# Two pairs of experts summed in one accumulation group, and expert weights loaded as runs of consecutive rows

## The chip, the cores and the metric

The kernel runs on one core of a Trainium2 chip. The metric is the device time of one execution in microseconds (us), with all inputs in HBM at the start and the output in HBM at the end. Three runs of the kernel before took 1796.16, 1798.23 and 1798.26 us; the median is 1798.23.

## The reference

The kernel computes two transformer blocks over 512 tokens of width 1024 in float32. The change touches the mixture of experts at the end of the first block. Cut to what matters, it is:

```python
def hierarchical_moe(h, w_rg, b_rg, w_re, b_re, w_gate, w_up, w_down):
    xt = h.reshape(512, 1024)
    ...                                   # top-1 group of 4, then top-2 of its 8 experts
    def expert_block(args):               # rows of one expert: 1024 -> 512 -> 1024
        toks, e = args
        xb = x_pad[toks]
        hid = jax.nn.silu(xb @ w_gate[e]) * (xb @ w_up[e])
        return hid @ w_down[e]
    ...
    out = out.at[tok_buf].add(y * w_buf)  # each token: the sum over its two experts
```

The kernel reads every expert's three matrices (2 MiB each, 192 MiB in all) once. `h` is the RMS norm of the residual `x` with gain `ffn_norm_g`, and the result is added to `x`.

## The kernel before, in words

The kernel is one stream of work built in program order for five engines. TensorE's order is fixed by `chained` (L154): every matmul is tied behind the one emitted before it. Weights and other inputs are loaded by DMAs that SyncE issues in order.

The stage of the experts runs from about 303 us to 814 us of the profile. The 32 experts are taken as 16 pairs, numbered p = 0 to 15, and two pairs (p even, then p odd) share one one-hot matrix and one gathered input. Each expert has 64 slots for tokens. The steps of a pair are methods of the class `Experts`:

- `dispatch` (L1096) gathers the tokens of two pairs by multiplying the residual rows, held as a high part `xh` and a low part `xl`, with the one-hot matrix `oh`. It is done in two halves of 512 features, each evicted by VectorE with the norm's gain.
- `gate` (L1132) and `up` (L1155) multiply the gathered input with the expert's weights. Expert 0 of the pair uses columns 0 to 63 of TensorE's array and expert 1 columns 64 to 127, in plain float32, so two matmuls run side by side. Each has 8 chunks k of 128 input features.
- `hidden` (L1165): ScalarE makes the silu of the gate from PSUM (through `act`, L188), and VectorE multiplies it with the up part (L1169) into `sg`.
- `turn` (L1171) transposes `sg` on TensorE into `hT`; `down` (L1179) multiplies it with the down weights, and ScalarE and VectorE split the result into a high and a low part (`split`, L143).
- `prepare` (L1138) transposes the next pair's one-hot into `ohT` and collects its token weights.
- `adds` (L1190) scatters a pair's rows back: for each of 8 chunks m of output features two matmuls of the full 128x128 array with `ohT`, and one VectorE addition into the residual `x1T` (L1199).

The main loop (L1438) interleaves them. While pair p runs its `up`, the eight adds of pair p-1 are dropped in one at a time after chunks 1 to 7 of the up sweep, and the eighth behind it. Between `hidden` and `turn`, and between `turn` and `down`, TensorE is given other work (`fill`): the next pair's gate in two halves if p is even, the two halves of the next dispatch if p is odd, and for p = 15 two adds each time. The adds of the last pair run after a test for overflowing experts (L1468).

The expert weights are loaded 1 MiB at a time into a ring of 13 tiles (`ring`, L879), which reuses all of the kernel's weight buffers. A load can be issued once the matmuls that read the tile's last contents are done. `load_up` (L889) gives partition p of chunk k the input row 128 k + p of the expert, a run of 2 KB; `load_down` (L894) likewise, with runs of 4 KB. `got_o` (L927) makes `xh` and `xl` before the stage, on ScalarE (L953) and GpSimd (L958).

Of the kernel before, what the change touches and what calls it, by code (L numbers as in the profile page):

```python
# [18 lines left out]
P = 128  # L19
# [20 lines left out]
def _program(tc, nc, es, I, out):  # L40
# [20 lines left out]
    def a4(shape, dt=F32):  # L61
        return ap_.tile(shape, dt, tag="a", name=nm("a"))
# [16 lines left out]
    def b32(ap):  # L79
        return ap.bitcast(F32)  # L80
# [253 lines left out]
    for g in range(4):  # L334
        nc.sync.dma_start(w_r[:, :, 4 + 8 * g:12 + 8 * g],
                          I["w_router_expert"][0, g].rearrange("(k p) e -> p k e", p=P))
    b_r = rp_.tile([P, 36], F32, name="b_r")
    nc.sync.dma_start(b_r[:, 0:4], I["b_router_group"][0].partition_broadcast(P))
    nc.sync.dma_start(b_r[:, 4:36], I["b_router_expert"][0].rearrange("g e -> (g e)").partition_broadcast(P))

# [545 lines left out]

    wg_d, wu_d, wd_d = I["w_gate"][0], I["w_up"][0], I["w_down"][0]

    def load_up(src, e, half):  # L889
        w = wtile([P, 4, FF])  # L890
        nc.sync.dma_start(w, src[e, half * 512:(half + 1) * 512, :].rearrange("(k p) f -> p k f", p=P))
        return w

    def load_down(e, half):  # L894
        w = wtile([P, 2, D])
        nc.sync.dma_start(w, wd_d[e, half * 256:(half + 1) * 256, :].rearrange("(k p) f -> p k f", p=P))
        return w

    def loads():
# [13 lines left out]
    emb_d = dr.tile([P, NT, D], F32, name="emb_d")  # L913

    ss1 = tm.tile([P, NT, 4], F32, name="ss1", bufs=1)
    xh, xl, x1T = [], [], []
    lt_ps = pvb()
    posts = []

# [7 lines left out]
    def got_o(g, c2, ps):  # L927
        xx = xt[g][:, 2 * c2:2 * c2 + 2, :]
        V.tensor_tensor(xx, xx, ps, op=ALU.add)

        def post():
            if len(x1T) == g:
                x1T.append(a4([P, 2, S]))
                xh.append(a4([P, NT, 256], F32R))
                xl.append(a4([P, NT, 256], F32R))
            ts = slice(c2 * 256, c2 * 256 + 256)
            pt = tr((P, 2, 256))
            for k in range(2):
                for ci in range(2):
                    tpose(pt[:, k, ci * P:(ci + 1) * P], xt[g][:, 2 * c2 + ci, k * P:(k + 1) * P])  # L940
            xr[:] = [tm.tile([P, 2, 256], F32R, tag=t, name=nm("xr"), bufs=b) for t, b in (("ohT", 2), (("sg", "hT")[c2], 1))]
            hi = nc.scalar.activation(xr[0], pt, AF.Copy)
            V.tensor_tensor(xr[1], pt, b32(xr[0]), op=ALU.subtract)
            cs = slice(2 * c2, 2 * c2 + 2)
            rest, last_ = [], (g, c2) == (3, 1)
            for ci in range(2):
                c = 2 * c2 + ci
                junk = tm.tile([P, 256], F32, tag="junk", name=nm("junk"), bufs=1)
                rest.append(nc.scalar.activation(junk, xt[g][:, c, :], AF.Square, accum_out=ss1[:, c, g:g + 1]))
            if last_:  # L950
                rms1()
            more = [nc.scalar.activation(x1T[g][:, :, ts], pt, AF.Copy),
                    nc.scalar.activation(xh[g][:, cs, :], xx, AF.Copy)]  # L953
            for i_ in rest:
                tc.add_manual_dep(i_.ins, hi.ins.name, no_sync, reason="order")
            for i_ in more:
                tc.add_manual_dep(i_.ins, rest[-1].ins.name, no_sync, reason="order")
            i_ = nc.gpsimd.tensor_tensor(xl[g][:, cs, :], xx, b32(xh[g][:, cs, :]), op=ALU.subtract)  # L958
            if last_:
# [136 lines left out]
    def dispatch(oh, nsl, XT):  # L1096

        per = 512 // nsl if nsl >= 128 else 4  # L1100
        for half in range(2):
            X = a4([P, 4, nsl])
            for k0 in range(0, 4, per):
                ps = mm((P, per, nsl))
                for kk in range(per):
                    k = half * 4 + k0 + kk
                    for c in range(NT):
                        mmul(ps[:, kk, :], xh[k // 2][:, c, (k % 2) * P:(k % 2 + 1) * P], oh[:, c, :], c == 0, False)
                        mmul(ps[:, kk, :], xl[k // 2][:, c, (k % 2) * P:(k % 2 + 1) * P], oh[:, c, :], False, c == NT - 1)
                k = half * 4 + k0  # L1110
                V.tensor_tensor(X[:, k0:k0 + per, :], ps,
                                gffn[:, k:k + per, :].broadcast_to([P, per, nsl]), op=ALU.mult)
            XT.append(X)
            yield

    class Experts:


        def __init__(self, XT, s0, ne, wg, wu, wd, oh_pair, g_of, after=None):
            self.XT, self.s0, self.ne, self.n = XT, s0, ne, ne * SLOTS  # L1120
            self.wg, self.wu, self.wd, self.oh, self.g_of, self.after = wg, wu, wd, oh_pair, g_of, after
            self.rows = []

        def _up(self, ps, w, ks):
            for k in ks:
                for e in range(self.ne):
                    s0 = self.s0 + 64 * e
                    mmul(ps[64 * e:64 * e + 64, :], self.XT[k // 4][:, k % 4, s0:s0 + 64], w()[e][k // 4][:, k % 4, :],
                         k == 0, k == KD - 1)
                yield  # L1130

        def gate(self, ks=range(KD)):  # L1132
            if ks[0] == 0:
                self.gps = mm()
            for _ in self._up(self.gps, self.wg, ks):
                pass

        def prepare(self):  # L1138

# [15 lines left out]
        def up(self, between=()):  # L1155

            between = list(between)
            self.ups = mm()
            for k, _ in enumerate(self._up(self.ups, self.wu, range(KD))):
                if k and between:  # L1160
                    between.pop(0)()
            for f in between:
                f()
# [26 lines left out]
        def adds(self):  # L1190

            def add(m):
                def f():
                    ps = mm()
                    ms = slice((m % 4) * P, (m % 4 + 1) * P)
                    for t in range(2):
                        mmul(ps, self.rows[m // 4][0:self.n, t, ms], self.ohT[0:self.n], t == 0, t == 1)
                    xx = x1T[m // 2][:, m % 2, :]
                    V.tensor_tensor(xx, xx, ps, op=ALU.add)  # L1199
                    if self.after:  # L1200
                        self.after(m)
                return f

            return [add(m) for m in range(KD)]


    it = rt([1])
# [1 line left out]
    def overflow():  # L1209
# [30 lines left out]
        def dyn(src, r0, nr):  # L1240
            n = src.shape[2]
            w = wm.tile([P, nr // P, n], F32, tag="wm", name=nm("wm"))
            nc.sync.dma_start(w, src[bass.ds(e_reg, 1), r0:r0 + nr, :].rearrange("e (k p) f -> p (e k) f", p=P))
            return w

        wg = [[dyn(wg_d, 0, 512), dyn(wg_d, 512, 512)]]
        wu = [[dyn(wu_d, 0, 512), dyn(wu_d, 512, 512)]]
        wd = [[dyn(wd_d, 0, 256), dyn(wd_d, 256, 256)]]
        XT = []
        for _ in dispatch(oh, SLOTS, XT):  # L1250
            pass
# [4 lines left out]
        x.hidden()  # L1256
        x.turn()
        x.down()
        for f in x.adds():
            f()  # L1260
        V.tensor_scalar(it, it, 1.0, None, op0=ALU.add)

# [160 lines left out]
    def pair(p, XT, oh):  # L1423
# [4 lines left out]
        return Experts(XT, sl.start, 2, wg, wu, wd, ohf[:, :, sl], lambda c: Ghl[:, c, p, :],  # L1428
                       row_done if p == N_PAIRS - 1 else None)

    pe_chain.append(None)
    XT = []
# [4 lines left out]
    adds = []  # L1437
    for p in range(N_PAIRS):  # L1438

        last = p == N_PAIRS - 1  # L1440
# [19 lines left out]
        if not last:  # L1460
            if p % 2:
                nxt.gate()
            nxt.prepare()
            x = nxt
    pe_chain.clear()

    st.load(1)
# [624 lines left out]
```

## Time and profile before

| | |
|---|---|
| median of 3 runs | 1798.23 us |
| profiled execution, its own time | 1798.43 us |
| its span, first to last instruction | 1796.3 us |
| TensorE busy in the span | 1741.2 us (97%) |
| VectorE, ScalarE, GpSimd busy | 899.8, 669.4, 322.8 us |
| HBM read | 308.13 MB, 174 GB/s over the span |
| mean granted clock of TensorE | 0.995 of full speed |

The profile is of one execution. In its rows PE is TensorE's matmuls, PEld its weight loads (which run beside the matmuls), DVE VectorE, ACT ScalarE, POOL GpSimd and SP SyncE. A matmul's duration there contains the time in which it passes through the array, so matmuls overlap, and the pace is read from one start to the next. A float32 matmul of the experts is recorded as two. A share of DMA above 1 means that packets of one DMA engine overlapped in the records.

### The profile page before, as it was taken

How to read it: one execution, taken by the hardware profiler on the slowest of the kernel's cores; microseconds unless marked ns; L12 is line 12 of the kernel's file. 1: busy time of each engine (PE TensorE's matmuls, PEld its weight loads, DVE VectorE, ACT ScalarE, POOL GpSimd, SP SyncE). 2: the span in 40 equal slices, each digit the busy share in tenths (PEclk: the TensorE clock that was granted, in tenths of full speed). 3: DMA queues.
4: the chain of work that ended last, by engine and by line, in shares of the span. 5: the costliest groups of instructions: out<-in, count | busy, mean ns of one | idle time of the engine just before them, and what ended most of it. 6: DMA issues, size and time to landing. Idle time of an engine off the chain costs nothing.

```text
span 1796.3 us, 22703 instructions
## 1 busy us (share of the span) xinstructions
PE 1741.2 (97%) x9108; PEld 1239.2 (69%) x9108; DVE 899.8 (50%) x1423; ACT 669.4 (37%) x1182; POOL 322.8 (18%) x273
## 2 busy tenths in 40 slices
PE   8999899999999999998999998999999999999998
PEld 5888688444434434436788786777888888888888
DVE  5456764223323323236666368888545543434356
ACT  5234544001010010114666168878523431323234
POOL 5352322000000000004533034333022000000033
PEclk9999999999999999999999999999999999999999
DMA  5322337999999999983222322211233222232331
GB/s 149 95 71 74 115 130 260 375 382 385 394 392 389 390 391 389 386 333 109 94 71 88 106 77 66 75 54 53 94 105 94 94 94 94 94 94 94 118 117 48
DMA packets 205071, 315.92 MB, mean 176 GB/s; under 512 B 14114, under 2 KB 119332, under 8 KB 204964
## 3 DMA queue, kind: packets, MB, share of 16 engines
q1 hardware_dynamic: 204244, 311.82, 49.3%
q0 software_dynamic: 576, 2.10, 0.3%
q8 instruction: 73, 1.20, 0.3%
q10 hardware_dynamic: 144, 0.52, 0.1%
q14 instruction: 34, 0.28, 0.0%
HBM read 308.13 MB, written 4.19 MB: 174 GB/s over the span
## 4 chain that ended last, share of the span: by engine, by line
PE 40%; DVE 8%; ACT 4%; issue 2%; POOL 0%; POOLq 0%; DVEq 0%; ACTq 0%
PE mm L163 38%; DVE su L1797 2%; DVE ab L1794 1%; ACT ab L188 1%; PE sc L163 1%; DVE su L1798 1%; DVE wl L260 1%; DVE a L148 1%; ACT wh L259 1%; DVE ah L1818 0%; ACT af L188 0%; ACT ab L1791 0%; ACT a L1834 0%; PE pv L163 0%; ACT kt L1755 0%
## 5 line engine op out<-in xcount | busy, mean ns | idle before, releaser
L163 PE MATMUL mm<-a,wh 128*128 128x512 f32 x1568 | 496.5, 398 | 1.5 <-DVE eg L1704 0.9
L163 PEld LDWEIGHTS mm<-a,wh 128*128 128x128 f32 x1568 | 292.2, 190 | 67.3 <-issue 3.8
L163 PE MATMUL mm<-a,wl 128*128 128x512 f32 x784 | 308.7, 394 | 0.0
L259 ACT ACTIVATE wh<-w 128x512 fp32r<-128x512 f32 (+2 forms) x183 | 188.3, 1053 | 290.2 <-PE mm L163 240.8
L163 PE MATMUL mm<-wh,a 128*128 128x256 f32 (+1 forms) x1240 | 294.2, 330 | 0.2 <-DVE a L146 0.2
L260 DVE TENSOR_TENSOR wl<-w,wh 128x512 fp32r<-128x512 f32 (+2 forms) x127 | 204.3, 1615 | 68.1 <-ACT wh L259 67.6
L163 PE MATMUL mm<-wl,a 128*128 128x256 f32 (+1 forms) x704 | 228.5, 353 | 0.0
L163 PEld LDWEIGHTS mm<-wh,a 128*128 128x128 f32 (+1 forms) x1240 | 192.0, 182 | 22.4 <-issue 20.4
L163 PE MATMUL mm<-xp,wh 128*128 128x512 f32 x640 | 201.8, 396 | 0.0
L163 PEld LDWEIGHTS mm<-a,wl 128*128 128x128 f32 x784 | 148.0, 189 | 33.3 <-DVE wl L260 0.4
L163 PE MATMUL mm<-wm,a 128*64 128x512 f32 x536 | 150.9, 604 | 0.0
L163 PEld LDWEIGHTS mm<-xp,wh 128*128 128x128 f32 x640 | 120.1, 188 | 29.9 <-issue 0.5
L163 PEld LDWEIGHTS mm<-wl,a 128*128 128x128 f32 (+1 forms) x704 | 121.9, 177 | 22.8 <-issue 20.9
L1199 DVE TENSOR_TENSOR a<-a,mm 128x512 f32<-128x512 f32 x128 | 86.1, 685 | 101.7 <-PE mm L163 101.6
L163 PE MATMUL mm<-xp,wl 128*128 128x512 f32 x320 | 126.2, 394 | 0.0
L260 POOL TENSOR_TENSOR wl<-w,wh 128x512 fp32r<-128x512 f32 x56 | 81.0, 1452 | 227.3 <-ACT wh L259 217.4
L163 PEld LDWEIGHTS mm<-ohT,a 128*128 128x128 f32 x256 | 39.7, 188 | 90.3 <-DVE a L1199 47.9
L1177 ACT ACTIVATE hT<-tr 128x512 f32<-128x512 f32 x16 | 9.6, 599 | 248.0 <-PE tr L172 248.0
L148 DVE SCALAR_TENSOR_TENSOR a<-yp,wsl,a 128x512 fp32r<-128x512 f32 x32 | 24.0, 750 | 149.5 <-ACT a L144 149.5
L260 POOL TENSOR_TENSOR a<-w,a 128x1024 fp32r<-128x1024 f32 x1 | 3.1, 3082 | 514.3 <-ACT a L259 514.3
L163 PE MATMUL mm<-ohT,a 128*128 128x512 f32 x256 | 88.3, 440 | 3.1 <-DVEq L1469 2.4
L1344 POOL TENSOR_TENSOR a<-a,a 128x512 f32<-128x512 f32 x15 | 26.0, 1733 | 352.8 <-ACT a L1342 352.5
(427 smaller groups left out, 2569.8 us busy)
## 6 DMA issues: line engine op xcount, KB each, us to landing
wm<-in_w_gate_dram SPq DMA_DIRECT2D x36, 1024.0 KB
wm<-in_w_down_dram SPq DMA_DIRECT2D x35, 1024.0 KB
wm<-in_w_up_dram SPq DMA_DIRECT2D x31, 1024.0 KB
w<-in_w_in_dram SPq DMA_DIRECT2D x30, 1024.0 KB
w<-in_w_mlp_up_dram SPq DMA_DIRECT2D x16, 1024.0 KB
w<-in_w_mlp_down_dram SPq DMA_DIRECT2D x16, 1024.0 KB
w<-in_w_up_dram SPq DMA_DIRECT2D x14, 1024.0 KB
wl<-in_w_gate_dram SPq DMA_DIRECT2D x11, 1024.0 KB
```

Of the source, the lines that this page charges most:

```text
L148: nc.vector.scalar_tensor_tensor(lo, src, scale, b32(hi), op0=ALU.mult, op1=ALU.subtract)
L163: i = nc.tensor.matmul(ps, lhs, rhs, start=start, stop=stop, skip_group_check=more).ins
L188: ins = nc.scalar.activation(out_, in_, func, **kw).ins
L259: self.last = nc.scalar.activation(wh, w, AF.Copy)
L260: eng.tensor_tensor(wl, w, b32(wh), op=ALU.subtract)
L1177: nc.scalar.activation(self.hT[:, :, 0:n], tp[:, :, 0:n], AF.Copy)
L1199: V.tensor_tensor(xx, xx, ps, op=ALU.add)
L1344: nc.gpsimd.tensor_tensor(sq2[0][:, 0, :], sq2[0][:, 0, :], t, op=ALU.add)
L1794: V.scalar_tensor_tensor(ab, z, 0.0, ab, op0=ALU.max, op1=ALU.add)
L1797: V.tensor_tensor_scan(su[:, ::-1], ab[:, ::-1], ab[:, ::-1], 0.0, op0=ALU.add, op1=ALU.max)
L1798: V.tensor_tensor(su, z, su, op=ALU.subtract)
```

## The change

Four things are done together.

1. The method `adds` becomes a function `sums` over a list of pairs. For p = 1, 3, ..., 13 the rows of both pairs of the group are added in one go, behind the next pair's gate: eight accumulation groups in a row, each of four matmuls (two for either pair), and one VectorE addition for each. `up` runs without anything between its chunks. Pair 14 is added in the two fills of pair 15 (four adds each), and pair 15 after the test for overflow as before.
2. `load_up` gives partition p four consecutive rows of the expert's half matrix, one run of 8 KB, and `load_down` two consecutive rows, also 8 KB. Chunk k then holds the rows 4 p + k.
3. To match that, `xh` and `xl` are stored with the features in the new order, read with a step of four elements in `got_o`; a second copy `gffn4` of the gain is loaded in that order by one more small DMA; and `hidden` reads both PSUM banks with a step of four elements, so that the chunks of `sg` match the new down rows.
4. `overflow` follows (it does not run with these inputs, as the profile has no adds of it).

```diff
+    gffn4 = cp.tile([P, KD], F32, name="gffn4")
+    nc.sync.dma_start(gffn4.rearrange("p (h k) -> p h k", k=4), I["ffn_norm_g"][0].rearrange("(h p k) -> p h k", p=P, k=4))
...
     def load_up(src, e, half):
         w = wtile([P, 4, FF])
-        nc.sync.dma_start(w, src[e, half * 512:(half + 1) * 512, :].rearrange("(k p) f -> p k f", p=P))
+        nc.sync.dma_start(w, src[e, half * 512:(half + 1) * 512, :].rearrange("(p k) f -> p k f", p=P))
...
-        nc.sync.dma_start(w, wd_d[e, half * 256:(half + 1) * 256, :].rearrange("(k p) f -> p k f", p=P))
+        nc.sync.dma_start(w, wd_d[e].rearrange("(p k) f -> p k f", p=P)[:, 2 * half:2 * half + 2, :])
...
+            xp = xx.rearrange("p c (j k) -> p c k j", k=4)
+            js = slice(64 * (g % 2), 64 * (g % 2) + 64)
...
-                    nc.scalar.activation(xh[g][:, cs, :], xx, AF.Copy)]
+                    nc.scalar.activation(xh[hc][:, :, :, js], xp, AF.Copy)]
...
-            i_ = nc.gpsimd.tensor_tensor(xl[g][:, cs, :], xx, b32(xh[g][:, cs, :]), op=ALU.subtract)
+            i_ = nc.gpsimd.tensor_tensor(xl[hc][:, :, :, js], xp, b32(xh[hc][:, :, :, js]), op=ALU.subtract)
...
-            act(self.sg[0:n], self.gps[0:n], AF.Silu, scale=rsl)
-            V.scalar_tensor_tensor(self.sg[0:n], self.ups[0:n], rsl, self.sg[0:n], op0=ALU.mult, op1=ALU.mult)
+            by_chunk = lambda t: t[0:n].rearrange("p (j k) -> p k j", k=4)
+            sg = self.sg[0:n].rearrange("p (k j) -> p k j", k=4)
+            act(sg, by_chunk(self.gps), AF.Silu, scale=rsl)
+            V.scalar_tensor_tensor(sg, by_chunk(self.ups), rsl, sg, op0=ALU.mult, op1=ALU.mult)
...
-                    for t in range(2):
-                        mmul(ps, self.rows[m // 4][0:self.n, t, ms], self.ohT[0:self.n], t == 0, t == 1)
+                for i, x in enumerate(xs):
+                    for t in range(2):
+                        mmul(ps, x.rows[m // 4][0:x.n, t, ms], x.ohT[0:x.n], i + t == 0, i == len(xs) - 1 and t == 1)
...
-            rest, adds = adds[4:], adds[:4]
-            fill = [lambda: [f() for f in rest[:2]], lambda: [f() for f in rest[2:]]]
-        x.up(adds)
+            rest = sums([before])
+            fill = [lambda: [f() for f in rest[:4]], lambda: [f() for f in rest[4:]]]
+        x.up()
...
-        adds = x.adds()
         if not last:
             if p % 2:
                 nxt.gate()
+                for f in sums([before, x]):
+                    f()
             nxt.prepare()
```

On TensorE, in an even pair before, the up sweep (into the bank mm_3841, from weight tiles wm) is cut by adds (ohT) from its second chunk on:

```order
L163 MATMUL mm_3841<-wm_3769,a_3687 64x512
L163 MATMUL mm_3841<-wm_3771,a_3687 64x512
L163 MATMUL mm_3841<-wm_3769,a_3687 64x512
L163 MATMUL mm_3841<-wm_3771,a_3687 64x512
L163 MATMUL mm_3854<-ohT_3609,a_3785 128x512 x2
L163 MATMUL mm_3841<-wm_3769,a_3687 64x512
L163 MATMUL mm_3841<-wm_3771,a_3687 64x512
L163 MATMUL mm_3860<-ohT_3609,a_3785 128x512 x2
```

Every add of two matmuls stands alone there, between two matmuls of 64 columns on either side.

On TensorE after the change, at the end of the gate of pair 2 (bank mm_3770), the sums of pairs 0 (ohT_3502) and 1 (ohT_3611) follow:

```order
L163 MATMUL mm_3770<-wm_3634,a_3701 64x512
L163 MATMUL mm_3770<-wm_3636,a_3701 64x512
L163 MATMUL mm_3795<-ohT_3502,a_3596 128x512 x2
L163 MATMUL mm_3795<-ohT_3611,a_3755 128x512 x2
L163 MATMUL mm_3801<-ohT_3502,a_3596 128x512 x2
L163 MATMUL mm_3801<-ohT_3611,a_3755 128x512 x2
L163 MATMUL mm_3807<-ohT_3502,a_3596 128x512 x2
L163 MATMUL mm_3807<-ohT_3611,a_3755 128x512 x2
```

This goes on to the eighth bank: 32 matmuls of the full array stand in one block between the gate and the transposes of `prepare`, and the up sweep behind them has none left.

On VectorE before, the adds of a pair (L1199) stand around the product of `hidden` (sg):

```order
L1199 TENSOR_TENSOR a_2987<-a_2987,mm_3878 128x512
L1199 TENSOR_TENSOR a_2987<-a_2987,mm_3884 128x512
L1169 SCALAR_TENSOR_TENSOR sg_3898<-mm_3841,wsl_3832,sg_3898 128x512
L1199 TENSOR_TENSOR a_3103<-a_3103,mm_3890 128x512
L1199 TENSOR_TENSOR a_3103<-a_3103,mm_3894 128x512
```

After the change `hidden` (L1171 there) stands behind the small reductions of `prepare`, with no add near it:

```order
L1202 TENSOR_TENSOR a_3107<-a_3107,mm_3831 128x512
L1202 TENSOR_TENSOR a_3107<-a_3107,mm_3837 128x512
L1156 TENSOR_REDUCE wsl_3850<-tr_3851 128x1
L1159 TENSOR_REDUCE wsl_3850<-tr_3851 64x1 x2
L1171 SCALAR_TENSOR_TENSOR sg_3884<-mm_3859,wsl_3850,sg_3884 128x512
L148 SCALAR_TENSOR_TENSOR a_3936<-yp_3919,wsl_3850,a_3936 128x512
```

The additions number 8 for two pairs where they numbered 16.

## Rows read from the trace of the kernel before

**Rows 1.** The page, busy time of each engine over the span.

```profile
PE 1741.2 (97%) x9108; PEld 1239.2 (69%) x9108; DVE 899.8 (50%) x1423; ACT 669.4 (37%) x1182; POOL 322.8 (18%) x273
```

**Rows 2.** Waits of PEld, 302 to 815 us: total us, times, longest us.

```profile
PEld mm L163 <- issue: 136.4, 397, 0.8
...
PEld yp L163 <- DMA w<-in_w_up_dram: 0.3, 1, 0.3
```

**Rows 3.** Stretches: us, busy us by engine, TensorE clock, DMA share, GB/s.

```profile
302.00:797.00 495.00, 494.13 (x2418) 213.99 (x2418) 148.51 (x271) 50.87 (x81) 0.53 (x1) 1.00 1.03 387
465.00:475.00 10.00, 10.00 (x49) 3.62 (x46) 3.60 (x7) 2.55 (x4) 0.00 (x0) 1.00 1.03 409
480.00:495.00 15.00, 15.00 (x96) 10.71 (x98) 6.08 (x9) 0.60 (x1) 0.00 (x0) 1.00 1.05 385
795.00:800.00 5.00, 5.00 (x22) 1.47 (x20) 1.56 (x4) 0.00 (x0) 0.00 (x0) 1.00 0.67 267
```

**Rows 4.** Timeline of PE, an even pair's up with adds: start us, us, what.

```profile
507.28 1.94 PE L163 MATMUL mm<-wm,a 128*64 128x512 f32 x8
509.14 0.73 PE L163 MATMUL mm<-ohT,a 128*128 128x512 f32 x2
509.81 1.08 PE L163 MATMUL mm<-wm,a 128*64 128x512 f32 x4
510.82 0.74 PE L163 MATMUL mm<-ohT,a 128*128 128x512 f32 x2
...
519.18 1.20 PE L163 MATMUL mm<-ohT,a 128*128 128x512 f32 x4
520.32 3.65 PE L163 MATMUL mm<-wm,a 128*64 128x512 f32 x16
523.90 0.65 PE L172 MATMUL tr<-ident,sg 128*128 128x128 f32 x4
```

**Rows 5.** Timeline of PE, a gate sweep without adds.

```profile
757.51 7.04 PE L163 MATMUL mm<-wm,a 128*64 128x512 f32 x32
764.48 0.66 PE L172 MATMUL tr<-ident,a 128*128 128x128 f32 x4
```

**Rows 6.** The longest unbroken run of full matmuls, in the chain that ended last.

```profile
1402.47 337.77 PE mm L163 x1472
```

**Rows 7.** Timeline of PE, pair 15, from its up to its down.

```profile
793.99 1.94 PE L163 MATMUL mm<-wm,a 128*64 128x512 f32 x8
...
805.28 0.66 PE L172 MATMUL tr<-ident,sg 128*128 128x128 f32 x4
805.70 1.18 PE L163 MATMUL mm<-ohT,a 128*128 128x512 f32 x4
806.81 0.64 PE L163 MATMUL yp<-wh,hT 128*64 128x512 f32 x1
```

**Rows 8.** The adds on VectorE, from the page's costliest groups (xcount, busy us, mean ns).

```profile
L1199 DVE TENSOR_TENSOR a<-a,mm 128x512 f32<-128x512 f32 x128 | 86.1, 685 | 101.7 <-PE mm L163 101.6
```

**Rows 9.** Timeline of SP, two issues of down tiles, and the last expert load.

```profile
459.44 0.88 SPq L896 DMA_DIRECT2D w<-in_w_down_dram  x2
...
786.29 0.37 SPq L896 DMA_DIRECT2D wl<-in_w_down_dram  x1
```

**Rows 10.** The product of hidden: ns min/median/max, first and last start.

```profile
L1169 DVE SCALAR_TENSOR_TENSOR sg<-mm,wsl,sg x16: 749/751/752, 327.1 to 804.5; 128x512 f32<-128x512 f32 x16
```

**Rows 11.** Timeline of DVE, a reduction with a step of 8 elements, one without.

```profile
297.48 0.40 DVE L1066 TENSOR_REDUCE rt<-rt 128x32 f32<-128x128 f32 x1
...
305.18 0.41 DVE L1404 TENSOR_REDUCE rt<-ov 128x32 f32<-128x256 f32 x1
```

**Rows 12.** The low parts on GpSimd, and where TensorE first reads them.

```profile
L958 POOL TENSOR_TENSOR a<-a,a x8: 1275/1290/1754, 254.6 to 294.4; 128x512 fp32r<-128x512 f32 x8
...
303.46 4.29 PE L163 MATMUL mm<-a,a 128*128 128x256 f32 x32 [0.87 <-DVE a L1363]
```

**Rows 13.** Timeline of SP, an issue of the small loads at the start.

```profile
23.45 0.65 SPq L335 DMA_DIRECT2D w_r<-in_w_router_expert_dram  x1
```

More of the change, by code (lines that the diff above doesn't have):

```diff
@@ L915, in _program @@
     ss1 = tm.tile([P, NT, 4], F32, name="ss1", bufs=1)
-    xh, xl, x1T = [], [], []
+    xh, xl, x1T = {}, {}, []
     lt_ps = pvb()
@@ L933, in post @@
                 x1T.append(a4([P, 2, S]))
-                xh.append(a4([P, NT, 256], F32R))
-                xl.append(a4([P, NT, 256], F32R))
+            hc = (g // 2, c2)
+            if hc not in xh:
+                xh[hc] = a4([P, 2, 4, P], F32R)
+                xl[hc] = a4([P, 2, 4, P], F32R)
+            xp = xx.rearrange("p c (j k) -> p c k j", k=4)
+            js = slice(64 * (g % 2), 64 * (g % 2) + 64)
             ts = slice(c2 * 256, c2 * 256 + 256)
@@ L1105, in dispatch @@
                 for kk in range(per):
-                    k = half * 4 + k0 + kk
                     for c in range(NT):
-                        mmul(ps[:, kk, :], xh[k // 2][:, c, (k % 2) * P:(k % 2 + 1) * P], oh[:, c, :], c == 0, False)
-                        mmul(ps[:, kk, :], xl[k // 2][:, c, (k % 2) * P:(k % 2 + 1) * P], oh[:, c, :], False, c == NT - 1)
+                        mmul(ps[:, kk, :], xh[half, c // 2][:, c % 2, k0 + kk, :], oh[:, c, :], c == 0, False)
+                        mmul(ps[:, kk, :], xl[half, c // 2][:, c % 2, k0 + kk, :], oh[:, c, :], False, c == NT - 1)
                 k = half * 4 + k0
                 V.tensor_tensor(X[:, k0:k0 + per, :], ps,
-                                gffn[:, k:k + per, :].broadcast_to([P, per, nsl]), op=ALU.mult)
+                                gffn4[:, k:k + per].unsqueeze(2).broadcast_to([P, per, nsl]), op=ALU.mult)
             XT.append(X)
@@ L1116, in _program, with __init__ @@
     class Experts:
-        def __init__(self, XT, s0, ne, wg, wu, wd, oh_pair, g_of, after=None):
+        def __init__(self, XT, s0, ne, wg, wu, wd, oh_pair, g_of):
             self.XT, self.s0, self.ne, self.n = XT, s0, ne, ne * SLOTS
-            self.wg, self.wu, self.wd, self.oh, self.g_of, self.after = wg, wu, wd, oh_pair, g_of, after
+            self.wg, self.wu, self.wd, self.oh, self.g_of = wg, wu, wd, oh_pair, g_of
             self.rows = []
@@ L1129, in _up @@
                          k == 0, k == KD - 1)
-                yield
         def gate(self, ks=range(KD)):
@@ L1134, in gate @@
                 self.gps = mm()
-            for _ in self._up(self.gps, self.wg, ks):
-                pass
+            self._up(self.gps, self.wg, ks)
         def prepare(self):
@@ L1153, in prepare, with up @@
                 V.tensor_reduce(self.wsl[sl, 0:1], wps[sl, 2 * e:2 * e + 2], axis=AX.X, op=ALU.add)
-        def up(self, between=()):
-            between = list(between)
+        def up(self):
             self.ups = mm()
[L1159 to L1163, printed above, removed]
+            self._up(self.ups, self.wu, range(KD))
         def hidden(self):
@@ L1188, in down, with sums, add, f @@
                 self.rows.append(y)
[L1190 to L1195, printed above, removed]
-                    for t in range(2):
-                        mmul(ps, self.rows[m // 4][0:self.n, t, ms], self.ohT[0:self.n], t == 0, t == 1)
[L1198 to L1204, printed above, removed]
+    def sums(xs, after=None):
+        def add(m):
+            def f():
+                ps = mm()
+                ms = slice((m % 4) * P, (m % 4 + 1) * P)
+                for i, x in enumerate(xs):
+                    for t in range(2):
+                        mmul(ps, x.rows[m // 4][0:x.n, t, ms], x.ohT[0:x.n], i + t == 0, i == len(xs) - 1 and t == 1)
+                xx = x1T[m // 2][:, m % 2, :]
+                V.tensor_tensor(xx, xx, ps, op=ALU.add)
+                if after:
+                    after(m)
+            return f
+        return [add(m) for m in range(KD)]
     it = rt([1])
@@ L1238, in overflow, with dyn @@
         e_reg = nc.sync.value_load(ei[0:1, 0:1], min_val=0, max_val=N_EXPERTS - 1)
[L1240 to L1243, printed above, removed]
-            return w
-        wg = [[dyn(wg_d, 0, 512), dyn(wg_d, 512, 512)]]
-        wu = [[dyn(wu_d, 0, 512), dyn(wu_d, 512, 512)]]
-        wd = [[dyn(wd_d, 0, 256), dyn(wd_d, 256, 256)]]
+        def dyn(src, half):
+            w = wm.tile([P, 4, FF] if src.shape[1] == D else [P, 2, D], F32, tag="wm", name=nm("wm"))
+            src = src[bass.ds(e_reg, 1), :, :]
+            if w.shape[1] == 4:
+                src = src[:, 512 * half:512 * half + 512, :].rearrange("e (p k) f -> p (e k) f", p=P)
+            else:
+                src = src.rearrange("e (p k) f -> p (e k) f", p=P)[:, 2 * half:2 * half + 2, :]
+            nc.sync.dma_start(w, src)
+            return w
+        wg, wu, wd = [[[dyn(src, half) for half in range(2)]] for src in (wg_d, wu_d, wd_d)]
         XT = []
@@ L1258, in overflow @@
         x.down()
-        for f in x.adds():
+        for f in sums([x]):
             f()
@@ L1427, in pair @@
         sl = slice(2 * j * SLOTS, (2 * j + 2) * SLOTS)
-        return Experts(XT, sl.start, 2, wg, wu, wd, ohf[:, :, sl], lambda c: Ghl[:, c, p, :],
-                       row_done if p == N_PAIRS - 1 else None)
+        return Experts(XT, sl.start, 2, wg, wu, wd, ohf[:, :, sl], lambda c: Ghl[:, c, p, :])
     pe_chain.append(None)
@@ L1436, in _program @@
     x.prepare()
-    adds = []
     for p in range(N_PAIRS):
@@ L1462, in _program @@
                 nxt.gate()
+                for f in sums([before, x]):
+                    f()
             nxt.prepare()
-            x = nxt
+            before, x = x, nxt
+    adds = sums([x], row_done)
     pe_chain.clear()
```

## The prediction

> **What bounds the kernel now.** I read the page first: TensorE is busy for 97% of the span and no other engine for more than half [rows 1], so the question is what TensorE does in the stage of the experts and whether anything makes it wait. The waits of that stage come next. TensorE's weight loads stood 0.3 us for a DMA, once, and 136.4 us in 397 pieces of at most 0.8 us under "issue", where no other engine is named [rows 2]. So the weights are always there in time, and the loss is in many small gaps of TensorE's own.
>
> The stretches show how close the second bound is. From 302 to 797 us TensorE is busy throughout at full clock, and the DMA share is 1.03: the loads run without a pause too, at 387 GB/s on average [rows 3]. There are two levels within: 409 GB/s from 465 to 475 us and 385 GB/s from 480 to 495 us [rows 3]. The loads move in order of issue, and the first stretch lies a few loads behind down tiles issued at 459.44 [rows 9], so I take it for their runs of 4 KB and the second for gate and up tiles with runs of 2 KB. So the loads are fast enough today, with little to spare. If TensorE gets faster, the rate decides how much of it is seen.
>
> The timeline shows where the gaps are. A gate sweep with nothing in it takes 764.48 - 757.51 = 6.97 us for its 16 float32 matmuls, 0.436 each [rows 5]. An up sweep has as many, but with the eight adds it takes 520.32 - 507.28 = 13.04 us [rows 4]. The adds of one pair thus cost 6.07 us, 0.76 per add. Their two matmuls alone would take 0.46: the longest unbroken run of such matmuls has 1472 in 337.77 us, 0.2295 each [rows 6]. The rest shows in one period: from one add to the next, 509.14 to 510.82, are 1.68 us, of which 0.46 are the add and 0.87 the two float32 matmuls [rows 4]. The 0.35 left over belong to the two changes between matmuls of 64 columns and of 128, 0.175 us a change.
>
> **The change part by part.** The profiled execution took 1798.43 us, 0.2 above the median of the runs; the sum is made against it.
>
> *Adds out of the up sweeps.* Pairs 1 to 14 lose all eight adds from their sweep: 14 x 6.07 = 85.0 us.
>
> *Sums in a row.* Seven blocks of 32 matmuls come in behind a gate: 32 x 0.2295 + one change of 0.175 = 7.52 us each, 52.6 us in all. Here I rely on the long run's pace. The nearest short run is slower: in pair 15 four such matmuls take 805.70 to 806.81, 1.11 us or 0.278 each with the change inside [rows 7]. That is the upper bound; no row of this shape is faster than 0.2295, so it is the lower one too. I take 0.2295 because a block of 32 is nearer to a run than to a piece of four. What could stop it is the bank: each group of four matmuls (0.92 us) ends in a VectorE addition of 0.685 us [rows 8], and three of the four banks are free, the fourth holding the next gate. The addition is shorter than its group, so it stays hidden. For 16 adds 8 additions remain; VectorE is busy for 148.51 of 495 us there [rows 3], so the ones saved are worth nothing by themselves.
>
> *Pair 15.* It had four adds in the sweep and four in the fills: 793.99 to 806.81, 12.82 us [rows 7]. Now it has a bare sweep (6.97), eight adds in the fills (16 x 0.2295 = 3.67, one change 0.175) and the transposes between (805.28 to 805.70, 0.42): 11.24 us, 1.6 less.
>
> Sum on TensorE: 85.0 - 52.6 + 1.6 = 34.0 us, if nothing else becomes late.
>
> *Loads of 8 KB.* The instructions and their order on SyncE stay as they are; the runs grow from 2 and 4 KB to 8. The loads must keep up with a TensorE that ends 34 us sooner. Between 302 and 797 us they moved 387 x 495 = 191.6 MB; in the last window the rate falls off [rows 3], which adds some 0.5 MB and puts the end near 798.3, for a load issued at 786.29 [rows 9]. That tile is first read two chunks into the last down, 806.81 + 4 x 0.436 = 808.6 [rows 7]: 10 us to spare. After the change it is read at 774.6, so 192.1 MB must move in 472.6 us: 406 GB/s. The trace has no run of 8 KB. Its bounds from the nearest rows: no better than today's mixture without its dips, (2 parts at 385, 1 at 409) 393 GB/s, or as far above 409 as a fixed cost per run allows. For one of 16 DMA engines 2 KB take 85.1 ns and 4 KB 160.2, so 75.1 per 2 KB and 10 fixed; 8 KB would take 310 ns, 422 GB/s. I take 422, since both rows lie on that line; 409 would do as well (771.7, 3 us early). The DMA cover is gone below 406.
>
> The Trainium skill speaks against a gain here: "DMA: Bandwidth & Descriptors", section Specifications, gives 512 B as the shortest transfer that reaches line rate, so by it 2, 4 and 8 KB should be equally fast. The two levels of this trace differ by 6% between 2 and 4 KB, which the rule would not give. By the rule the sum would be that of the first rival below, by the rows it is the forecast.
>
> *Strided reads in `hidden`.* ScalarE reads the gate's bank long before it is needed. VectorE's product takes 0.75 us [rows 10]; the transposes of `sg` come 523.90 - 520.32 = 3.58 us after the sweep [rows 4], behind half a gate (half a dispatch in odd pairs). The trace shows no PSUM read with such a step. Bounds: no loss, or what a strided read of SBUF costs: a reduction over 128 elements with a step takes 0.40 us where one over 256 without takes 0.41 [rows 11], so at most about twice. The product would then take 1.5 us, hidden in 3.58, and in pair 15 too, whose fill is now 2.0 us. I take zero; it costs from about 3.5 us on. A gain is excluded, since nothing is left out.
>
> *Reordered `xh`, `xl`.* GpSimd's eight subtractions take 1.29 us, the last from 294.4; TensorE reads them from 303.46 on [rows 12], 7.8 us later. ScalarE's copies lie before them. Even tripled they fit: zero, with a few us as the other end. *The extra load of the gain* costs SyncE one issue like its neighbour's 0.65 us, ahead of the next weight load [rows 13]: 0 to 0.65, and I take zero, since TensorE has work then.
>
> All together 1798.43 - 34.0 = 1764.5 us.
>
> **The rivals.**
>
> *The loads become the bound.* If longer runs bring nothing, as that page's rule has it, the loads run at 393 GB/s: 192.1 MB end at 302 + 489 = 791, 16 us after TensorE wants the last tile: 1781 us. For it: a DMA share of 1.03 leaves no room [rows 3]. Against it: 409 against 385 for twice the run. This is also the case in which that part of the change does not do what it says.
>
> *The block runs at the pace of pair 15's short pieces.* With 0.278 instead of 0.2295 for 240 matmuls, 11.6 us less 1.4 for the eight changes contained, the gain is 24: 1775 us. For it: each group waits for a bank freed by VectorE. Against it: 0.685 is less than 0.92.
>
> *Strided PSUM reads become a wait.* Then TensorE stands before the transposes of `sg`, 16 times. The gain is used up when VectorE's product takes 3.5 + 34.0/16 = 5.6 us, over seven times the 0.75 of today. At eight times (6.0) it is 16 x 2.5 = 40 us: 1804 us, slower than before. For it there is no row; the step of rows 11 gives a factor of two. The Trainium skill ("SBUF — State Buffer", the section on the DMA port swizzle, in its remark on cachelines) says that PSUM has lines of 8 bytes and that access out of sequence slows matmuls significantly; a step of 16 bytes meets a new line each time. It gives no factor, and no row here shows one.
>
> **How the numbers follow.** Forecast, TensorE bound with the loads in time: 0.79, at 1764.5, its own range 1760 to 1770 (a change less in the seven even sweeps that run straight into a gate, 1.2 us; small waits up to 5). Loads as the bound: 0.11, 1781. Slow block: 0.07, 1775. Strided reads: 0.03, 1804. The range that leaves out no more than 2 in 10 runs from 1760 to 1780, by way of the two rivals on the same side. About 0.2% (3.6 us) can be told from no change by a measurement of this kernel; both nearer rivals stay clear of that, so faster has 0.95, slower 0.03 and the same 0.02 (a rival between its bounds).
>
> **What would show it.** Right: up sweeps of 7 us in all pairs; blocks of 32 matmuls with `ohT` of 7.3 to 7.6 us; a DMA rate of about 420 GB/s or, if more, dips in it; no DMA named before a weight load of TensorE; the last down ending near 780 us. Wrong: blocks of 9 us with VectorE's additions named; a stage with DMA waits before gate or up and a steady rate under 406; `sg` above 3.5 us; or anything behind the stage that is not simply moved forward by 34 us.

## The result and the profile after

The changed kernel takes 1773.93 us (median of 4 runs, 1770.95 to 1775.92) against 1798.24 (1796.16 to 1798.33) for the kernel before: a ratio of 0.9866, 95% interval [0.9849, 0.9883]. It is 24.3 us faster where 34.0 were forecast, inside the stated range of 1760 to 1780 and 9.4 us above the forecast.

The page of the changed kernel gives the busy time of each engine, to stand beside [rows 1]:

```profile
PE 1721.1 (97%) x9108; PEld 1260.7 (71%) x9108; DVE 865.9 (49%) x1367; ACT 673.9 (38%) x1182; POOL 322.9 (18%) x273
```

TensorE has the same 9108 matmuls in 20 us less, VectorE has 56 additions fewer, and TensorE is still busy for 97% of the span. The timeline of TensorE after the change, from the gate of pair 2 over the block and the up sweep behind it to the transposes of `sg`:

```profile
367.56 7.04 PE L163 MATMUL mm<-wm,a 128*64 128x512 f32 x32
374.52 7.74 PE L163 MATMUL mm<-ohT,a 128*128 128x512 f32 x32
382.10 0.60 PE L172 MATMUL tr<-ident,a 128*128 128x128 f32 x4
382.45 0.59 PE L163 MATMUL tr<-rt,a 128*128 128x6 f32 x4
382.97 3.65 PE L163 MATMUL mm<-wm,a 128*64 128x512 f32 x16
...
393.42 0.66 PE L172 MATMUL tr<-ident,sg 128*128 128x128 f32 x4
```

The block takes 382.10 - 374.52 = 7.58 us where 7.52 were worked out. From 382.97 to 393.42 there are 10.45 us, one up sweep and half a gate at 6.97 us a sweep: the sweep of 13.04 us in [rows 4] is gone. In pair 15 the adds of pair 14 now stand in the two fills; the first four of them take 774.67 - 772.71 = 1.96 us:

```profile
772.71 2.13 PE L163 MATMUL mm<-ohT,a 128*128 128x512 f32 x8
774.67 0.60 PE L172 MATMUL tr<-ident,sg 128*128 128x128 f32 x4
```

The loads keep up. Three stretches of the changed kernel (columns as in [rows 3]):

```profile
307.00:775.00 468.00, 468.00 (x2438) 231.47 (x2438) 113.00 (x213) 50.28 (x80) 0.00 (x0) 1.00 0.99 410
465.00:475.00 10.00, 10.00 (x59) 5.18 (x58) 2.12 (x6) 1.51 (x3) 0.00 (x0) 1.00 1.01 423
480.00:495.00 15.00, 15.00 (x73) 5.44 (x73) 2.19 (x3) 1.38 (x2) 0.00 (x0) 1.00 1.01 418
```

At 8 KB a run the levels are 423 and 418 GB/s where [rows 3] had 409 and 385; 422 was the estimate. What TensorE's weight loads waited for in the stage (us in total, times, longest):

```profile
PEld mm L163 <- issue: 143.4, 473, 0.8
PEld yp L163 <- issue: 68.6, 240, 0.4
...
PEld mm L163 <- DMA wm<-in_w_up_dram: 0.7, 4, 0.2
PEld mm L163 <- DMA wm<-in_w_down_dram: 0.6, 2, 0.3
PEld mm L163 <- DMA wh<-in_w_up_dram: 0.3, 2, 0.2
```

No wait for a DMA is longer than 0.3 us. The stage of the experts, from the first dispatch (303.46 before, 306.57 after) to the last adds (816.34 and 786.59), went from 512.88 to 480.02 us: 32.9 less of the 34.0 forecast. By the spans of the two profiled runs (1796.3 and 1773.9; that of the changed kernel is the slowest of its four) 10.5 us were lost outside, where the change was priced at zero: 3.1 before the stage, 2.7 between the start of the last adds and the first matmul with weights of the next stage, and 4.7 spread over all that follows. In that last part the longest run of matmuls, in the chain that ended last, stands like this, against 337.77 in [rows 6]:

```profile
1376.93 340.86 PE mm L163 x1472
```

The matmuls are the same, the granted clock is 1.00 throughout, and nothing is waited for, but from one start to the next are 231.6 ns on average instead of 229.5.

### The profile page after: what moved, and what is told of

Read it like the earlier page. It is cut to its first block, busy times and chain, and to the rows that moved or that the text cites. A ratio compares the mean times of both kernels' runs of the same rounds, so it can differ in the third digit from the quotient of the medians.

```text
span 1773.9 us, 22564 instructions
## 1 busy us (share of the span) xinstructions
PE 1721.1 (97%) x9108; PEld 1260.7 (71%) x9108; DVE 865.9 (49%) x1367; ACT 673.9 (38%) x1182; POOL 322.9 (18%) x273
## 4 chain that ended last, share of the span: by engine, by line
PE 41%; DVE 7%; ACT 4%; issue 2%; POOL 1%; POOLq 0%; DVEq 0%; ACTq 0%
PE mm L163 39%; DVE su L1802 2%; DVE ab L1799 1%; PE sc L163 1%; ACT ab L188 1%; DVE wl L260 1%; DVE su L1803 1%; ACT wh L259 1%; DVE a L148 1%; PE pv L163 1%; DVE ah L1823 0%; ACT af L188 0%; ACT ab L1796 0%; ACT kt L1760 0%; ACT a L1839 0%
## 5 line engine op out<-in xcount | busy, mean ns | idle before, releaser
L163 PE MATMUL mm<-wl,a 128*128 128x256 f32 (+1 forms) x704 | 224.5, 352 | 0.0
L163 PEld LDWEIGHTS mm<-wh,a 128*128 128x128 f32 (+1 forms) x1240 | 196.3, 183 | 25.1 <-issue 23.1
L163 PE MATMUL mm<-wm,a 128*64 128x512 f32 x536 | 139.1, 595 | 0.0
L163 PEld LDWEIGHTS mm<-wm,a 128*64 128x64 f32 x536 | 42.7, 137 | 67.9 <-issue 66.4
L1946 DVE TENSOR_TENSOR a<-a,mm 128x512 f32<-128x512 f32 x40 | 27.4, 685 | 105.4 <-PE mm L163 105.4
L144 ACT ACTIVATE a<-yp,wsl 128x512 fp32r<-128x512 f32 x32 | 22.0, 688 | 147.4 <-PE yp L163 147.4
L1202 DVE TENSOR_TENSOR a<-a,mm 128x512 f32<-128x512 f32 x72 | 48.6, 685 | 59.6 <-PE mm L163 59.6
```

The source lines that it names most:

```text
L144: i = nc.scalar.activation(hi, src, AF.Identity, scale=scale)
L163: i = nc.tensor.matmul(ps, lhs, rhs, start=start, stop=stop, skip_group_check=more).ins
L1946: V.tensor_tensor(xch(m), xch(m), ps, op=ALU.add)
```

## The experiments

Two theories stood against each other for the 10.5 us. *Placement*: the tile `gffn4` takes 32 bytes per partition at the end of the pool `cp`, so the tiles `a` and `w` and the later tiles on that side start 32 bytes further along, and TensorE's pace depends on where its operands start. *Drift*: the pace differs by execution, and nothing in the change causes it. Other runs take the change apart.

**The changed kernel again** (no edit).

> The changed kernel once more, timed in turn with the kernel before on one chip, as the yardstick of the other runs. Of the 34.0 us that TensorE was to save, 24.3 were seen; the profile shows 32.9 us saved within the stage of the experts and some 10 lost outside of it, 2.7 of them between the end of the last pair and the last adds, the rest spread over runs of full-array matmuls that take 233 ns each where they took 229.6. Placement theory: the 32 bytes per partition of gffn4 push every tile allocated later 32 bytes along, and the pace of matmuls depends on where their tiles start; then the triple of ns is there in every execution: again about 1774 us. Drift theory: the pace differs from one execution or chip to the next; then this run may come out anywhere from 1765 to 1776, and in its profile the pace of the long run of 1472 matmuls is nearer to 229.6 than to 233.

1774.58 us (ratio to before 0.9866, [0.985, 0.9881]), the stage 480.0 us, and the long run as before:

```profile
1376.45 340.85 PE mm L163 x1472
```

The triple of ns repeats too: over much of the run the starts lie 231, 231 and 238 ns apart, again and again. Drift is out, since the second execution is as slow as the first in the same places.

**The tile padded to 128 bytes.**

```
-gffn4 = cp.tile([P, KD], F32, name="gffn4")
+gffn4 = cp.tile([P, 32], F32, name="gffn4")[:, 0:KD]
```

> The changed kernel with gffn4 as a tile of 128 bytes per partition, of which 32 are used: all later tiles start at the same place modulo 128 bytes as in the kernel before. Placement theory: the full-array matmuls of the long run are back at 229.6 ns, over some 2000 such matmuls behind the stage and as much time before it 5 to 9 us: about 1767 us. Drift theory, or the load itself as the cause: no change, about 1774 us.

1773.53 us, ratio 0.9858 [0.9843, 0.9874]: nothing gained. Its long run:

```profile
1376.03 341.10 PE mm L163 x1473
```

So what I had taken for the rule, the start modulo 128 bytes, was wrong (the run is counted one matmul longer here). But the matmuls of this kernel have a pattern of their own: over long stretches their starts lie some 231 and 236 ns apart in turn, 233 on average. That speaks for the place of the tiles, and does not show it.

**The tile and its load alone, in the kernel before.** The two lines of `gffn4` are added, and nothing reads it.

> The kernel before with the tile gffn4 and its load added and nothing else changed; the tile is not read. Placement theory: 5 to 9 us slower than the kernel before, about 1805 us, the long run of matmuls at 233 ns each. Drift theory: as the kernel before, 1798 us, or at most the one issue of 0.65 us more.

1805.81 us, ratio 1.0042 [1.0029, 1.0056]: 7.6 us slower than before, for a tile that nothing uses. Its long run:

```profile
1409.07 340.48 PE mm L163 x1472
```

The loss thus belongs to this tile and not to the sums or the expert loads. Whether it is its bytes or its load was left to the next run.

**The tile in another pool, its load kept.**

```
-gffn4 = cp.tile([P, KD], F32, name="gffn4")
+gffn4 = rp_.tile([P, KD], F32, name="gffn4")
```

> The changed kernel with gffn4 allocated in the pool rp, which lies behind the pools of the tiles a and w: these stand at exactly the addresses of the kernel before, while wm, ohT and sg stay 32 bytes further along. The load itself is kept. The pad of 128 bytes brought nothing (ratio to the changed kernel 0.999), but each of the kernels before, changed and padded showed its own repeating pattern of matmul durations in the long run: 232, 225, 230 ns before; 232, 237, 231 changed; 233, 233, 234 padded. Placement theory, with the exact address in place of the address modulo 128: the pattern 232, 225, 230 is back, the long run takes 338 us again in place of 341, and the kernel 5 to 7 us less: about 1768 us. Load theory (the extra load, or the shift of what follows it in the queues, sets the pace): no change, 1774 us, long run 341.

1765.22 us (1764.80 to 1766.34), ratio 0.9819 [0.9806, 0.9833]: 33.4 us faster than before, and the fastest kernel of this study. The long run is that of the kernel before to the hundredth:

```profile
1368.76 337.77 PE mm L163 x1472
```

Its mean granted clock is 0.993, as in the changed kernel, so the clock as a whole does not explain the difference. Its block of 32 is shorter too, 379.45 - 372.01 = 7.44 us:

```profile
372.01 7.61 PE L163 MATMUL mm<-ohT,a 128*128 128x512 f32 x32
379.45 0.60 PE L172 MATMUL tr<-ident,a 128*128 128x128 f32 x4
```

**The same kernel, its tiles moved on** by 32, 64 and 224 bytes. One tile that lies ahead of them is made longer, and nothing uses the added bytes; the program places tiles in steps of 32 bytes, so that 16 bytes more are a shift of 32. The tiles `wm`, `ohT` and `sg` move by the same distance:

```
-coef = cp.tile([P, 8], F32, name="coef")
+coef = cp.tile([P, 12], F32, name="coef")[:, 0:8]     # 24 and 64 in the other two
```

> The kernel of e5 (gffn4 in the pool rp) with one tile of cp made longer, so that the tiles a, w and xp stand 32 bytes further along, where they are in the changed kernel; nothing reads or writes the added bytes. Placement theory: the pattern 232, 237, 231 ns and the 341 us of the long run are back, and the time of the changed kernel, 1774 us. Rival (e5 was faster for another reason, the place of gffn4 itself or of its load): still 1765 us.

> The kernel of e5 with the tiles a, w and xp 64 bytes further along. If the place modulo 64 bytes decided, it would be as fast as e5, 1765 us; the padded kernel (128 bytes further, and slow) speaks against that. If every distance has a pattern of its own, the long run of 1472 matmuls takes anything from 330 to 345 us, the kernel 1755 to 1776; I expect 341 us and 1774.

> The kernel of e5 with the tiles a, w and xp 224 bytes further along, so that every tile a starts at a multiple of 1 KB. If a start on a large power of two is what the reads of TensorE like, this is the fastest place: under 335 us for the long run and under 1762 us for the kernel. If not, as the padded kernel: 341 us and 1774.

The long run of each, in this order:

```profile
1375.27 340.85 PE mm L163 x1472
```

```profile
1374.63 341.01 PE mm L163 x1472
```

```profile
1374.02 338.06 PE mm L163 x1472
```

1772.85 us (ratio 0.9855 [0.9837, 0.9873]), 1773.82 (0.9863 [0.9846, 0.9879]) and 1768.41 (0.9836 [0.9819, 0.9852]). The shift of 32 bytes alone brings the time and the pattern of the changed kernel back, so placement is shown as the cause. A start at a multiple of 1 KB is better than most, but not the fastest place, as I had guessed it might be. A rule for good places doesn't follow: of the starts 34592, 34624, 34656, 34720 and 34816 bytes of the first tile `a`, the first is fast, the last nearly so, and the three between are slow.

The long run does tell the tiles apart. TensorE multiplies there `a` in some stretches and `xp` in others with the weights in `wh` and `wl`, which stand at the same place in every kernel, and does not read `w`. Two stretches of 40 us, the first reading `a` and the second `xp`, in the kernel before, in the changed kernel, and in the one moved by 224 bytes (the first count is that of the matmuls):

```profile
1474.00:1514.00 40.00, 40.00 (x177) 32.81 (x176) 14.59 (x12) 7.10 (x6) 0.00 (x0) 1.00 0.33 105
1518.00:1558.00 40.00, 40.00 (x173) 32.20 (x172) 18.14 (x18) 14.42 (x18) 0.00 (x0) 1.00 0.31 102
```

```profile
1448.00:1488.00 40.00, 40.00 (x173) 32.17 (x172) 14.60 (x12) 7.26 (x6) 0.00 (x0) 1.00 0.31 98
1493.00:1533.00 40.00, 40.00 (x173) 32.20 (x172) 18.17 (x18) 14.42 (x18) 0.00 (x0) 1.00 0.31 102
```

```profile
1444.00:1484.00 40.00, 40.00 (x173) 32.15 (x172) 14.57 (x12) 7.31 (x6) 0.00 (x0) 1.00 0.30 98
1489.00:1529.00 40.00, 40.00 (x177) 32.81 (x176) 18.59 (x18) 14.45 (x18) 0.00 (x0) 1.00 0.32 105
```

The pace goes by the tile that is read. At some places a matmul starts every 228.9 ns, at the others every 232.3 to 234.3: before the change `a` had the fast pace and `xp` a slow one, after it both have a slow one, and 224 bytes on it is `xp` that has the fast one. The block of 32 does not follow `a` alone, however: in the kernel moved by 32 bytes it takes 7.45 us, as with the tile in the other pool.

**Weights of the dispatch read with a step.** With the padded tile, `xh` and `xl` stay in the order of the rows, and TensorE picks every fourth column when it loads them as weights:

```
-xh[hc] = a4([P, 2, 4, P], F32R)
+xh[hc] = a4([P, 2, 512], F32R)
...
-mmul(ps[:, kk, :], xh[half, c // 2][:, c % 2, k0 + kk, :], oh[:, c, :], c == 0, False)
+mmul(ps[:, kk, :], xh[half, c // 2][:, c % 2, k0 + kk::4], oh[:, c, :], c == 0, False)
```

> The kernel with the padded gffn4, and xh and xl kept in the order of the rows, so that ScalarE and GpSimd write and read them without a step, and TensorE loads the weights of the dispatch with a step of 16 bytes instead. Theory that the copies with a step cost (ScalarE 1126 instead of 621 ns, GpSimd 1548 instead of 1290): about 1.2 us faster than the padded kernel, with the waits of TensorE for these copies before the stage gone. Rival: the weight loads with a step are slower than their matmuls; the dispatches (8 of 64 matmuls, 512 in all) then take longer, by 27 us if a load takes 0.16 instead of the 0.11 us that a matmul of 256 columns covers.

1829.15 us, ratio 1.0181 [1.0167, 1.0195]. The rival was right, and by more than it said. The first dispatch of the padded kernel, and of this one:

```profile
305.61 4.30 PE L163 MATMUL mm<-a,a 128*128 128x256 f32 x32 [0.87 <-DVE a L1368]
```

```profile
304.06 7.71 PE L163 MATMUL mm<-a,a 128*128 128x256 f32 x32 [0.87 <-DVE a L1367]
```

A group of 32 takes 3.4 us more, and 16 such groups are 16 x 3.4 = 55 of the 59 us that its stage is longer. The run also prices the copies with a step. Its stage begins 305.61 - 304.06 = 1.55 us earlier, but 0.48 of that stands before the first of these copies: the same matmul of the router starts at 252.44 us in the padded kernel and at 251.96 in this one. That leaves 1.1 us. The copies of the changed kernel on ScalarE and on GpSimd (ns min/median/max, first and last start):

```profile
L962 ACT ACTIVATE a<-a x8: 1110/1126/1142, 255.5 to 296.5; 128x512 fp32r<-128x512 f32 x8
```

```profile
L967 POOL TENSOR_TENSOR a<-a,a x8: 1535/1548/1569, 256.7 to 297.7; 128x512 fp32r<-128x512 f32 x8
```

and the same copy on ScalarE where it has no step, in this experiment:

```profile
L961 ACT ACTIVATE a<-a x8: 617/620/623, 254.0 to 293.9; 128x512 fp32r<-128x512 f32 x8
```

**The sums without the long loads.** All hunks of the sums, and the loads and the layout of the kernel before:

```
-nc.sync.dma_start(w, src[e, half * 512:(half + 1) * 512, :].rearrange("(p k) f -> p k f", p=P))
+nc.sync.dma_start(w, src[e, half * 512:(half + 1) * 512, :].rearrange("(k p) f -> p k f", p=P))
```

> The sums of two pairs in a row, but the loads and the layout of the kernel before, with runs of 2 and 4 KB. Loads theory (the 8 KB runs are what lets TensorE's gain be seen): the loads move 192.1 MB at 393 GB/s or less, the stage of the experts is 489 us or longer instead of 480 and TensorE waits for weights: 1775 to 1785 us. Rival: TensorE sets the pace alone and the loads have slack, stage 480 us, and with the placement of the kernel before about 1765 us.

1785.02 us, ratio 0.9932 [0.9919, 0.9946]. TensorE waits, and for the expert weights:

```profile
PEld yp L163 <- DMA wm<-in_w_down_dram: 7.5, 5, 2.4
PEld yp L163 <- DMA wl<-in_w_down_dram: 4.8, 2, 2.4
...
PEld mm L163 <- DMA wm<-in_w_up_dram: 2.1, 3, 1.0
```

The whole of its stage, at a DMA share of 1.03:

```profile
300.00:790.00 490.00, 480.84 (x2441) 233.93 (x2439) 113.29 (x213) 50.35 (x80) 0.07 (x1) 1.00 1.03 391
```

The loads run at 391 GB/s and the stage takes 502.4 us. This is the prediction's first rival (393 GB/s, 1781 us), which comes about when the long runs are left out.

**The long loads without the sums.** The hunks of the loads and the layout alone; the adds stay in the up sweeps, as in the kernel before.

> The loads of 8 KB with the reordered xh, xl and hidden and gffn4, but the adds between the matmuls of the up sweeps as before. Theory that TensorE was the bound before: the loads bring nothing by themselves; 1805.8 us as with gffn4 alone, plus 1.2 us for the copies with a step: 1807 us. Rival, that the loads already held TensorE back before: clearly under 1803 us, the stage of the experts shorter than 512.9 us.

1807.63 us, ratio 1.0052 [1.0038, 1.0066]: 1.8 us above the kernel with the unused `gffn4`. Its stage takes 512.87 us, as before, and the DMA engines now have time to spare:

```profile
306.00:800.00 494.00, 493.94 (x2410) 213.69 (x2410) 148.06 (x267) 50.27 (x80) 0.39 (x1) 1.00 0.93 388
```

By itself this half of the change is a loss of 9.0 us, most of it that of the unused tile.

**The sums of each pair alone, still in a row.**

```
-for f in sums([before, x]):
+for f in sums([before]) + sums([x]):
```

> The changed kernel with the same block behind a gate, but the sums of the two pairs one after the other, 16 groups of two matmuls in 16 banks in a row instead of 8 groups of four. Theory that the four matmuls of a group (0.92 us) are what hides VectorE's addition (0.685 us): groups of 0.46 us run three ahead on the free banks and then go at VectorE's pace, the last of 16 begins 0.46 + 13 x 0.685 = 9.4 us after the first, a block takes 10.0 us or more instead of 7.6, 17 us or more in seven blocks: 1791 us or more. Rival, that only the change between matmuls of 64 and 128 columns counted and not the bank: no change, 1774 us.

1786.40 us, ratio 0.9935 [0.9922, 0.9949]: 12.5 us above the changed kernel. TensorE's block, VectorE's additions beside it, and the waits of the whole stage:

```profile
621.58 9.42 PE L163 MATMUL mm<-ohT,a 128*128 128x512 f32 x32
630.84 0.60 PE L172 MATMUL tr<-ident,a 128*128 128x128 f32 x4
```

```profile
622.35 9.66 DVE L1202 TENSOR_TENSOR a<-a,mm 128x512 f32<-128x512 f32 x16 [6.02 <-PE mm L163]
```

```profile
PEld mm L163 <- DVE a L1202: 22.1, 77, 0.3
```

The block takes 9.26 us, and TensorE waits for VectorE's additions, 77 times. The mechanism is the one expected, its size is not: I reckoned with 0.685 us an addition and 10.0 us a block, but additions in a row start (9.66 - 0.68) / 15 = 0.60 us apart, since the record of one reaches into the next. Seven blocks are 7 x (9.26 - 7.58) = 11.8 of the 12.5 us.

## Why the prediction was right, and where it was off

The measured time lies in the stated range, but outside the forecast's own 1760 to 1770. The range was drawn up to 1780 for two rivals that did not come about, so that it holds 1773.9 is luck; what is right is the sum on TensorE and the rate of the loads. Of the signs named beforehand the blocks, the bare sweeps and the DMA rate came as they should, and so did one of the signs of being wrong: what lies behind the stage did not simply move forward by 34 us.

*Adds out of the up sweeps, the blocks, pair 15.* Right: the block at 7.58 us (7.44 with the old placement) against 7.52, sweeps of 6.97, the stage 32.9 us shorter, and 512.88 - 479.07 = 33.8 in the kernel with the tile in the other pool, against 34.0. The addition stays hidden behind four matmuls, as said; the run with single pairs shows the case where it does not.

*Loads of 8 KB.* Right in direction and size. The line through the two older levels gave 422 GB/s, and 418 to 423 were measured. "The cover is gone below 406" agrees as far as it was tried: at 391 TensorE waited. The long loads are worth 1785.0 - 1765.2 = 19.8 us together with the sums and nothing without them (512.87 us of stage). The Trainium skill's rule ("DMA: Bandwidth & Descriptors", Specifications) that transfers are at line rate from 512 B on does not hold here: 391 GB/s for runs of 2 and 4 KB, 418 to 423 for 8 KB, in the same queue at a full DMA share.

*Strided reads in `hidden`.* Right: VectorE's product takes what it took in [rows 10], with 16 bytes from one element to the next:

```profile
L1171 DVE SCALAR_TENSOR_TENSOR sg<-mm,wsl,sg x16: 749/751/752, 330.2 to 772.9; 128x512 f32<-128x512 f32 x16
```

ScalarE's `Silu` is the same as well (688 ns, before 687). The warning of the Trainium skill ("SBUF — State Buffer", the remark on cachelines) that PSUM read out of sequence slows matmuls has no counterpart in these two engines' reads.

*Reordered `xh`, `xl`.* The term taken as zero was about 1 us: 1.1 by the run without the step, and 1.0 by the kernel with the tile in the other pool, whose stage begins 304.07 - 303.46 = 0.6 us later than before although it was 0.4 us ahead at the router matmul shortly before the first copy (251.29 and 251.71 us). The step does cost in SBUF: 1.8 times on ScalarE, 1.2 on GpSimd against [rows 12]. The remark on cachelines in the Trainium skill ("SBUF — State Buffer") has a penalty for each access that crosses to a new line of 16 bytes, and these copies agree; that 4 float32 can be stepped for free, as it says too, they do not bear out. I had looked for a cover only up to the dispatch, 7.8 us later, and that cover holds. But the slower copies also hold up work that TensorE needs before the dispatch, here in the changed kernel and then in the kernel before:

```profile
PEld pv L163 <- DVE xr L952: 3.2, 4, 1.4
```

```profile
PEld pv L163 <- DVE xr L943: 2.3, 3, 1.4
```

The beginning of the stage is a soft number in a single execution: with the sums alone, where nothing of the change lies ahead of the stage, it begins at 299.73 us, 3.7 us earlier than before.

*The extra load of the gain.* This is the step that failed. I priced its issue on SyncE, at 0 to 0.65 us, and not the tile: 1773.9 - 1765.2 = 8.7 us come with the 32 bytes by which it pushes others, and 1772.85 - 1765.22 = 7.6 came back with a shift of 32 bytes alone. With the tile in the other pool the whole change is worth 33.4 us, 0.6 less than the sum. Of the rivals, the slow block gave 1775 us, 1 us from the measured time, but for a reason that the block's 7.58 us exclude: agreement with a number alone would have named the wrong cause.

*What stays open.* Some of the loss is TensorE's clock after the last pair. The last adds of the changed kernel (DVEq is VectorE's instruction queue), and their stretch of 5 us:

```profile
786.59 3.97 PE L163 MATMUL mm<-ohT,a 128*128 128x512 f32 x10 [2.45 <-DVEq L1474]
792.49 2.67 PE L163 MATMUL mm<-ohT,a 128*128 128x512 f32 x6 [1.93 <-DVE a L1202]
```

```profile
785.00:790.00 5.00, 3.41 (x9) 2.74 (x10) 2.84 (x3) 4.51 (x5) 1.64 (x1) 0.66 0.00 2
```

The same in the kernel before:

```profile
816.34 2.57 PE L163 MATMUL mm<-ohT,a 128*128 128x512 f32 x10 [2.44 <-DVEq L1469]
819.55 1.92 PE L163 MATMUL mm<-ohT,a 128*128 128x512 f32 x6 [0.64 <-DVE a L1199]
```

```profile
815.00:820.00 5.00, 3.02 (x12) 2.10 (x12) 3.34 (x5) 4.97 (x6) 1.93 (x1) 1.00 0.01 2
```

Behind the same gap of 2.4 us the ten matmuls went in part at the lower of the two clocks (a mean of 0.66), where they had the full one before. The place of the tiles doesn't decide this alone. The kernel with the sums of single pairs has its tiles where the changed kernel has them, and shows the short form:

```profile
798.49 2.57 PE L163 MATMUL mm<-ohT,a 128*128 128x512 f32 x10 [2.45 <-DVEq L1474]
```

In the kernel with the tile in the other pool the ten matmuls slow down too, but the wait behind them is missing: from the start of the last adds to the first matmul with weights of the next stage it takes 803.26 - 783.14 = 20.1 us, the changed kernel 808.49 - 786.59 = 21.9, the kernel before 835.51 - 816.34 = 19.2. So 1.8 us of the difference between the first two lie here, and whether they are the clock's or the place's was not settled.

## What to carry to other kernels

When TensorE and the loads are both near their bound, price a change on the two together: here the sums alone gave 13.6 us, the long loads alone 9.0 us of loss (most of it the new tile's), and both 33.4 with the tiles left where they were. A group of matmuls whose bank an addition on another engine has to free should take longer than the distance of such additions in a row, and summing two pairs in one bank buys this. A new small tile belongs behind the tiles that the busiest engine reads, or has to be timed as an edit of its own.

## What the runs showed of the hardware that was not expected

- The place of a tile in its partition sets the pace of the matmuls of 128x512 that read it, at full clock (their operands are of type fp32r): one start every 228.9 ns at the fast places, every 232.3 to 234.3 at the others. A run of 1472 took 337.77 us at the first place, 338.06 at another, and 340.48 to 341.01 at three; at one and the same place three kernels agree within 0.4 us (340.48, 340.85, 340.86). For the whole kernel it is up to 8.7 us, 0.5%.
- A step of 16 bytes costs nothing in reads of PSUM by VectorE (751 ns) and ScalarE (688), 1.8 times in a read of SBUF by ScalarE; and matmuls of 256 columns whose weights are read with such a step start 0.23 us apart instead of 0.12.
- Additions of 128x512 in a row on VectorE start 0.60 us apart, though each is recorded with 0.68.
